# Down-projection of both gated layers by seven products instead of eight blocks, and another bank for the third pair

## The chip, the cores and the metric

One core of a Trainium2 chip runs the whole program. Its engines are a matrix engine (TensorE, PE in the rows, with PEld for its weight loads), VectorE (DVE), ScalarE (ACT), GpSimd (POOL), and SyncE (SP), which here only issues transfers. Each takes its own list of instructions in order. Transfers go through sixteen DMA engines. The metric is the time of one execution on the device, in microseconds.

## What is computed

A trunk of two layers over a sequence of 1024 rows of 1024 numbers, all in float32. Each layer is a mixer and then a gated feed-forward part; only the latter is changed:

```python
def conv_ffn(hn, w_in, conv_w, conv_b, w_out):      # D_FF = 2816
    a, u = jnp.split(hn @ w_in, 2, axis=-1)
    a = lax.conv_general_dilated(a, conv_w[:, None, :], ...) + conv_b   # causal, width 3
    return (jax.nn.silu(a) * u) @ w_out
...
h = h + mix(rmsnorm(h, norm_mix_g[layer]))
h = h + conv_ffn(rmsnorm(h, norm_ffn_g[layer]), ...)
return rmsnorm(h, final_norm_g)                      # after both layers
```

## The kernel before

**Precision.** Every float32 operand is split in two parts of a shorter type, hi on ScalarE (L129) and lo = x − hi on VectorE (L130). A product is then three matmuls (`mm3`, L161 to L163): hi·hi, hi·lo, lo·hi, each 128 x 128 stationary against 128 x 512 moving.

**Up-projection.** The 2816 columns are taken as 22 tiles of 128; for each, `Pair(f)` holds the a and the u half. It is one level of Strassen's scheme (seven products a11, s2, a12, s3, s1, a22, s4 instead of eight), each product four k times three matmuls. The weight's sums s1 to s4 are made by GpSimd (L880 to L886) in the loaded tile "raw"; each operand is then split into a tile of the ring "op" (six tiles of 1024 columns), three products ahead of use (`LOOK`). The results meet in three PSUM banks a pair, X, Y and Z; VectorE adds them up (L911, L915, L925, L932), convolves (L1068, L1070), ScalarE applies SiLU, and `tail` multiplies (L933 on VectorE, L934 on GpSimd) and writes the tile to `g_dram`. The first three pairs start early: while the second half of the rows is normalized and transposed, the matrix engine runs their a11 and a12. Their banks are written out by hand; bank 0 is X of pair 0 and also Z of pair 2.

**Down-projection.** The tiles of g are read back in groups of four (the first group two), split, and multiplied with the matching rows of w_out by `down`: for each group eight row blocks times two column halves, each block a PSUM bank "row" added into h by VectorE (L1092). In the last group the order is by row block, so that a block's two halves are done one after the other; in the last layer `final` then normalizes that row block and writes it out.

**Order.** A scheduler with a model of time lays out each engine's list; what it gives is shown below where it matters. SyncE's list holds all loads and writes of this stage.

Of the kernel before, what the change touches and what calls it, by code (L numbers as in the profile page):

```python
# [12 lines left out]
F32 = mybir.dt.float32  # L13
# [7 lines left out]
P = 128  # L21
# [23 lines left out]
LOOK = 3  # L45
EL, OL = (1, 2), (1, 3)
# [10 lines left out]
class Trunk:  # L57
# [11 lines left out]
    def weights(self, raw=0, bufs=0, size=1024):  # L69

        with self.tc.tile_pool(name="w", bufs=1, reuse_waits="tile") as w:
# [6 lines left out]
                "op": [base("whi", WBUFS) + base("wlo", WBUFS), 0],  # L78
# [742 lines left out]
    def ffn(self, L, h, pool, final=None):  # L821
# [10 lines left out]
        g_dram = tc.dram_tile([NF, P, S], F32, name="g_dram")  # L832
# [97 lines left out]
        def tail(p):  # L930
# [4 lines left out]
            nc.sync.dma_start(out=g_dram[p.f], in_=ct)  # L935
# [65 lines left out]
        ring = [[5, 3, 1, 6, 4, 2, 7, 0], 0]  # L1001
# [6 lines left out]
        for p, y, z in zip(early, (5, 6, 7), (3, 4, 0)):  # L1008
            p.banks = {"Y": y, "Z": z}
# [26 lines left out]
        for i, (p, name) in enumerate(steps):  # L1036
# [5 lines left out]
            run(p, name)  # L1042
            left[p.f] -= 1
# [4 lines left out]
        group = []  # L1048
        for f in range(0, NF, 2):
            gt = self.slot(("hn", "hn", "g", "g", "g")[f // 2 % 5], [P, 2, 2, S], F32R, name="g")  # L1050
            for m in range(2):
                ct = self.wtile("raw", F32) if f == 0 else pool.tile([P, S], F32, tag="ct", name="gr")
                nc.sync.dma_start(out=ct, in_=g_dram[f + m])
                self.split(gt[:, m, 0], gt[:, m, 1], ct)
            group += [(gt[:, m, 0], gt[:, m, 1]) for m in range(2)]
            done = f == NF - 2
            if len(group) == 4 or f == 0:
                f0 = f + 2 - len(group)
                self.down(h, group, w_out[f0 * P:(f + 2) * P], done, final() if done and final is not None else None)
                group = []  # L1060
# [12 lines left out]
    def down(self, h, x, w, last, final):  # L1073

        nc = self.nc
        nk = len(x)

        def chunks(col):
            cols = slice(col * HALF, (col + 1) * HALF)
            return [  # L1080
                self.weight(w[k0 * P:(k0 + 2) * P, cols].rearrange("(k p) n -> p k n", p=P)) for k0 in range(0, nk, 2)
            ]

        def block(half, t, col, wts):
            acc = self.bank(name="row")
            c0 = half * HALF + t * P
            for k in range(nk):
                self.mm3(
                    acc, [v[:, c0:c0 + P] for v in x[k]], [v[:, k % 2] for v in wts[k // 2]], k == 0, k == nk - 1
                )  # L1090
# [489 lines left out]
```

## Time and profile before

| | |
|---|---|
| median of 3 runs | 2330.0 us (2328.97 to 2330.22) |
| the profiled execution | 2328.61 us, span of its records 2326.6 us |
| PE busy | 2253.3 us, 97% |
| VectorE, ScalarE, GpSimd busy | 66%, 37%, 23% |
| DMA | 208.05 MB, mean 89 GB/s |

The two microseconds between execution and span lie before the first and behind the last record. The up-projections run from about 459 to 901 us and from 1623 to 2065 us, the down-projections from there to 1153 and 2312 us.

### The profile page before, as it was taken

The page shows a single profiled execution, that of the slowest core. Times are in us where ns is not written, and L with a number is a line of the kernel's source. Part 1 is how long each engine was busy: PE and PEld are TensorE (multiplying, and loading weights), DVE is VectorE, ACT ScalarE, POOL GpSimd, SP SyncE. Part 2 cuts the span into 40 slices and gives each one's busy share as a digit, 9 for nine tenths or more (in the row PEclk, how much of TensorE's full clock was granted, in tenths as well). Part 3 has the DMA queues.
Part 4 walks back from the last instruction along what each step waited for, and adds up shares of the span by engine and source line. Part 5 has one row for each costly group of instructions (what it writes and reads, how often), then busy time and mean ns, then how long its engine had stood idle before and what let it go on. Part 6 is the DMA issues. An engine that isn't in the chain of part 4 may idle for free. (4 is left out here: it accounts for less than half of the span.)

```text
span 2326.6 us, 29393 instructions
## 1 busy us (share of the span) xinstructions
PE 2253.3 (97%) x10945; PEld 1857.8 (80%) x10945; DVE 1541.0 (66%) x2627; ACT 860.9 (37%) x1498; POOL 535.1 (23%) x509
## 2 busy tenths in 40 slices
PE   7999999989999999999989999999899999999997
PEld 6777878868888887888888888887688888878886
DVE  6878895777666667544467777748776666665435
ACT  5454553443333333211234555545433333332112
POOL 0466410224444441000001000001344444410000
PEclk9999999989999999999999999999999999999999
DMA  6432323322222224321301000242222222243201
GB/s 195 126 106 80 105 91 109 127 64 82 82 82 82 82 82 159 130 92 61 113 10 45 30 31 27 109 156 73 64 90 81 80 81 80 83 169 127 91 28 73
DMA packets 196310, 208.05 MB, mean 89 GB/s; under 512 B 28289, under 2 KB 152393, under 8 KB 195657
## 3 DMA queue, kind: packets, MB, share of 16 engines
q1 hardware_dynamic: 196168, 206.19, 27.3%
q8 instruction: 86, 1.41, 0.2%
q14 instruction: 56, 0.45, 0.1%
HBM read 165.39 MB, written 39.58 MB: 88 GB/s over the span
## 5 line engine op out<-in xcount | busy, mean ns | idle before, releaser
L130 DVE TENSOR_TENSOR op<-raw,op 128x512 fp32r<-128x512 f32 x260 | 229.8, 886 | 213.3 <-ACT op L129 211.4
L161 PE MATMUL au<-bt,op 128*128 128x512 f32 x704 | 280.7, 399 | 16.7 <-DVE ct L933 12.4
L129 ACT ACTIVATE whi<-raw 128x1024 fp32r<-128x1024 f32 (+4 forms) x143 | 143.3, 1004 | 402.5 <-PE row L163 290.0
L162 PE MATMUL au<-bt,op 128*128 128x512 f32 x704 | 280.1, 398 | 1.4 <-DVE bt L130 1.4
L163 PE MATMUL au<-bt,op 128*128 128x512 f32 x704 | 279.6, 397 | 0.0
L162 PE MATMUL row<-wlo,g 128*128 128x512 f32 x704 | 275.8, 392 | 1.4 <-DVE wlo L130 1.3
L163 PE MATMUL row<-whi,g 128*128 128x512 f32 x704 | 274.8, 390 | 0.0
L129 ACT ACTIVATE op<-raw 128x512 fp32r<-128x512 f32 x260 | 163.0, 629 | 299.8 <-PE au L163 185.2
L161 PE MATMUL row<-whi,g 128*128 128x512 f32 x704 | 266.8, 393 | 1.3 <-DVE p L932 1.3
L130 DVE TENSOR_TENSOR wlo<-raw,whi 128x1024 fp32r<-128x1024 f32 (+4 forms) x143 | 171.7, 1201 | 114.3 <-ACT whi L129 113.7
L1092 DVE TENSOR_TENSOR h<-h,row 128x512 f32<-128x512 f32 x192 | 129.9, 684 | 173.5 <-PE row L163 173.2
L163 PE MATMUL au<-b,op 128*128 128x512 f32 x528 | 208.0, 394 | 1.1 <-DVE op L130 1.1
L161 PE MATMUL au<-b,op 128*128 128x512 f32 x528 | 208.0, 394 | 0.0
L162 PE MATMUL au<-b,op 128*128 128x512 f32 x528 | 207.9, 394 | 0.0
L161 PEld LDWEIGHTS au<-bt,op 128*128 128x128 f32 x704 | 133.5, 190 | 51.8 <-DVE ct L933 13.3
L162 PEld LDWEIGHTS au<-bt,op 128*128 128x128 f32 x704 | 133.7, 190 | 34.1 <-DVE bt L130 2.3
L163 PEld LDWEIGHTS au<-bt,op 128*128 128x128 f32 x704 | 133.6, 190 | 32.2
L161 PEld LDWEIGHTS row<-whi,g 128*128 128x128 f32 x704 | 132.1, 188 | 31.1 <-DVE p L932 2.2
L162 PEld LDWEIGHTS row<-wlo,g 128*128 128x128 f32 x704 | 132.2, 188 | 30.9 <-DVE wlo L130 2.9
L163 PEld LDWEIGHTS row<-whi,g 128*128 128x128 f32 x704 | 132.2, 188 | 29.8
L880 POOL TENSOR_TENSOR s<-raw 128x512 f32<-128x512 f32 x44 | 60.0, 1365 | 260.2 <-DMA raw<-in_ffn_w_in 229.0
L163 PEld LDWEIGHTS au<-b,op 128*128 128x128 f32 x528 | 99.0, 188 | 24.6 <-DVE op L130 1.4
(596 smaller groups left out, 4853.2 us busy)
## 6 DMA issues: line engine op xcount, KB each, us to landing
raw<-in_ffn_w_in SPq DMA_DIRECT2D x176, 256.0 KB, 3.1
g_dram<-ct SPq DMA_DIRECT2D x44, 512.0 KB, 3.4
raw<-in_ffn_w_out SPq DMA_DIRECT2D x44, 512.0 KB, 3.6
raw<-in_even_w_in SPq DMA_DIRECT2D x40, 512.0 KB, 3.8
gr<-g_dram SPq DMA_DIRECT2D x40, 512.0 KB, 3.2
h<-in_x SPq DMA_DIRECT2D x16, 512.0 KB, 10.4
raw<-in_even_w_out SPq DMA_DIRECT2D x16, 512.0 KB, 3.7
raw<-in_odd_w_out SPq DMA_DIRECT2D x16, 512.0 KB, 4.0
```

Of the source, the lines that this page charges most:

```text
L129: nc.scalar.activation(hi, src, AF.Copy)
L130: nc.vector.tensor_tensor(out=lo, in0=src, in1=hi.bitcast(F32), op=ALU.subtract)
L161: mm(out, l[0], r[0], start=start, stop=False, **how)
L162: mm(out, l[0], r[1], start=False, stop=False, **how)
L163: return mm(out, l[1], r[0], start=False, stop=stop, **how)
L880: tt(out=s.s1, in0=p("a21"), in1=p("a22"), op=ALU.add)
L1092: nc.vector.tensor_tensor(out=part, in0=part, in1=acc, op=ALU.add)
```

## The change

**Down-projection.** It becomes one level of the same scheme. g is cut by row halves (lo, hi) and by even and odd column tiles; w_out by even and odd row tiles and by column halves. Seven products take the place of eight blocks. Each runs over eleven steps q (two tiles f each), four row tiles t and the three matmuls of `mm3`: 132 matmuls and four banks. Four products accumulate on banks that others began; VectorE adds the banks to the quarters of h (L1153), 36 additions a layer.

**Operands of g.** `tail` now writes, for every two tiles, seven pieces of 128 x 512 to `g_dram`: three as they are and the sums s1 to s4 that VectorE makes (four operations of 128 x 512).

**Operands of w_out.** `turned(q)` loads two rows of tiles of 512 KB (buffers b1, which takes the place of the norm's gain row, and b2), makes four differences in place on VectorE (L964), and writes four pieces of 256 KB to a new DRAM tile `t_dram`. It is called eleven times in a layer, within the up-projection, in program order spread over its pairs (`TURN`).

**Streaming.** Each step of each product loads its two operands (256 KB each) into a half of a tile of a ring "row" and splits 128 x 1024 at once into one of fourteen units of memory; 77 such steps a layer. Nothing stays in memory from product to product.

**Buffers and banks.** The ring "op" has five tiles instead of six, since b2 takes one. Pair 2 has banks 5 and 7 instead of 7 and 0 for Y and Z, and the ring of banks for the pairs after it has another order.

**Final norm.** Its sums of squares are kept for each half and row tile, since the quarters of h are done in another order: the second half's left columns after the third product, the first half's two after the sixth, the second half's right columns after the seventh.

```diff
+TURN = (4, 6, 7, 8, 10, 12, 14, 15, 16, 18, 20)
...
-                "op": [base("whi", WBUFS) + base("wlo", WBUFS), 0],
+                "op": [base("whi", WBUFS) + base("wlo", WBUFS - 1), 0],
+                "row": [base("raw", WRAW) + more("raw+", raw) + base("whi", WBUFS) + base("wlo", WBUFS), 0],
...
-            nc.sync.dma_start(out=g_dram[p.f], in_=ct)
+            q, odd = p.f // 2, p.f % 2
+            put = lambda i, x: nc.sync.dma_start(out=g_dram[q, i], in_=x)
+            put(odd, ct[:, hi])
+            if not odd:
+                return
+            put(2, ct[:, lo])
+            even = pairs[p.f - 1].ct
+            s1, s2 = piece("p16", 2), piece("p16", 2)
+            V.tensor_tensor(out=s1, in0=even[:, lo], in1=ct[:, lo], op=ALU.add)
+            put(3, s1)
+            V.tensor_tensor(out=s2, in0=s1, in1=even[:, hi], op=ALU.subtract)
+            put(4, s2)
+            s3 = piece("s1", 2)
+            V.tensor_tensor(out=s3, in0=even[:, hi], in1=even[:, lo], op=ALU.subtract)
+            put(5, s3)
+            s4 = piece("u3", 1)
+            V.tensor_tensor(out=s4, in0=ct[:, hi], in1=s2, op=ALU.subtract)
+            put(6, s4)
+
+        def turned(q):
+
+            b1 = self.const.tile([P, S], F32, tag="gain", name="b1", bufs=1)
+            b2 = self.w.tile([P, S], F32, tag=f"wlo{WBUFS - 1}", name="b2", bufs=1)
+            for i, x in enumerate((b1, b2)):
+                nc.sync.dma_start(out=x, in_=w_out[(2 * q + i) * P:(2 * q + i + 1) * P])
+            sub = lambda out, x, y: V.tensor_tensor(out=out, in0=x, in1=y, op=ALU.subtract)
+            sub(b1[:, lo], b1[:, hi], b1[:, lo])
+            sub(b1[:, hi], b2[:, hi], b1[:, hi])
+            sub(b2[:, hi], b2[:, hi], b1[:, lo])
+            sub(b2[:, lo], b2[:, lo], b2[:, hi])
+            for i, x in enumerate((b1[:, lo], b2[:, hi], b1[:, hi], b2[:, lo])):
+                nc.sync.dma_start(out=t_dram[q, i], in_=x)
...
-        ring = [[5, 3, 1, 6, 4, 2, 7, 0], 0]
+        ring = [[3, 0, 6, 4, 1, 7, 5, 2], 0]
...
-        for p, y, z in zip(early, (5, 6, 7), (3, 4, 0)):
+        for p, y, z in zip(early, (5, 6, 5), (3, 4, 7)):
...
+            if name == "a12" and p.f in TURN:
+                turned(TURN.index(p.f))
...
-            if len(group) == 4 or f == 0:
-                f0 = f + 2 - len(group)
-                self.down(h, group, w_out[f0 * P:(f + 2) * P], done, final() if done and final is not None else None)
-                group = []
...
+        self.down(h, g_dram, t_dram, w_out, final() if final is not None else None)
...
-        if LASTMAJ and last:
-            both = [chunks(col) for col in range(2)]
-            for half in range(2):
-                for t in range(TB):
-                    for col in range(2):
-                        block(half, t, col, both[col])
-        else:
-            for col in range(2):
-                wts = chunks(col)
-                for half in range(2):
-                    for t in range(TB):
-                        block(half, t, col, wts)
...
+    def down(self, h, g, turned, w, final):
+
+
+        nc, tc = self.nc, self.tc
+        V = nc.vector
+        nq = NF // 2
+        low = [(x, n) for tag, k in (("hn", 2), ("g", 3)) for x in [tag] * k for n in range(2)]
+        own = [(f"b{i}", 0) for i in range(2, 6)]
+        units = {True: low + own, False: low[4:] + own}
+        held, at, last = {}, [0], []
+
+        def unit(free):
+
+            ring = units[free]
+            tag, n = ring[at[0] % len(ring)]
+            at[0] += 1
+            shape = [P, 2, 2, HALF]
+            if tag[0] == "b":
+                return self.xp.tile(shape, F32R, tag=tag, name="unit", bufs=1)
+            if n == 0:
+                held[0] = self.slot(tag, [P, 2] + shape[1:], F32R, name="unit")
+            return held[0][:, n]
+
+        def operands(q, a, b, free):
+            r = self.wtile("row", F32)
+            nc.sync.dma_start(out=r[:, :HALF], in_=g[q, a])
+            if isinstance(b, tuple):
+                src = w[(2 * q + b[0]) * P:(2 * q + b[0] + 1) * P, b[1] * HALF:(b[1] + 1) * HALF]
+            else:
+                src = turned[q, b]
+            nc.sync.dma_start(out=r[:, HALF:], in_=src)
+            u = unit(free)
+            flat = lambda x: x.rearrange("p s n -> p (s n)")
+            self.split(flat(u[:, 0]), flat(u[:, 1]), r)
+            return u
+
+        def product(banks, a, b, start, free, tail):
+            us = []
+            order = [(q, t) for q in range(nq - tail) for t in range(TB)]
+            order += [(q, t) for t in range(TB) for q in range(nq - tail, nq)]
+            for q, t in order:
+                while len(us) < min(nq, q + 9):
+                    us.append(operands(len(us), a, b, free))
+                u = us[q]
+                with tc.issue_after(last[0].ins) if last else nullcontext():
+                    mm = self.mm3(
+                        banks[t], [u[:, i, 0, t * P:(t + 1) * P] for i in range(2)], [u[:, i, 1] for i in range(2)],
+                        start and q == 0, q == nq - 1, skip_group_check=not start,
+                    )
+                last[:] = [mm]
+
+        def add(banks, *to, done=()):
+            for t in range(TB):
+                for half, col in to:
+                    x = h[half][:, t, col * HALF:(col + 1) * HALF]
+                    V.tensor_tensor(out=x, in0=x, in1=banks[t], op=ALU.add)
+                for half, col in done if final is not None else ():
+                    final(h[half], half, t, col)
+
+        banks = lambda: [self.bank(name="row") for _ in range(TB)]
+        X, Y = banks(), banks()
+        product(X, 0, (0, 0), True, True, 3)
+        add(X, (1, 1), (0, 0), (0, 1))
+        product(Y, 4, 1, True, True, 3)
+        add(Y, (1, 1))
+        product(X, 1, (1, 0), False, True, 3)
+        add(X, (1, 0), done=[(1, 0)])
+        product(Y, 5, 2, False, True, 3)
+        add(Y, (0, 1))
+        X = banks()
+        product(X, 3, 0, True, True, 3)
+        add(X, (0, 1))
+        product(Y, 2, 3, False, True, 3)
+        add(Y, (0, 0), done=[(0, 0), (0, 1)])
+        at[0] = 0
+        product(X, 6, (1, 1), False, False, 7)
+        add(X, (1, 1), done=[(1, 1)])
```

**What the lists look like.** VectorE's list about the third pair's first sums, in layer 0, before (L911 and L932 add a PE bank to a piece p, L130 splits an operand of the up-projection):

```order
L911 TENSOR_TENSOR p_4763<-p_4340,au 128x512
L130 TENSOR_TENSOR op<-raw,op 128x512
L1070 SCALAR_TENSOR_TENSOR ct<-ax,taps,ct 128x1024
L932 TENSOR_TENSOR p_4763<-p_4763,au 128x512
L130 TENSOR_TENSOR op<-raw,op 128x512
L933 TENSOR_TENSOR ct<-ct,au 128x512
L915 TENSOR_TENSOR u_4801<-p_4340,au 128x512
L130 TENSOR_TENSOR op<-s_4721,op 128x512
L130 TENSOR_TENSOR op<-raw,op 128x512
L925 TENSOR_TENSOR ax<-p_4340,au 128x512
```

and after (L915 and L936 are the same two additions, L964 is a difference of `turned`, its b a tile just loaded from w_out, L955 the last sum of `tail`):

```order
L955 TENSOR_TENSOR u_4757<-ct,p_4749 128x512
L964 TENSOR_TENSOR b_5980<-b_5980 128x512
L915 TENSOR_TENSOR p_4777<-p_4341,au 128x512
L936 TENSOR_TENSOR p_4777<-p_4777,au 128x512
L964 TENSOR_TENSOR b_5980<-b_5981,b_5980 128x512
L964 TENSOR_TENSOR b_5981<-b_5981,b_5980 128x512
L964 TENSOR_TENSOR b_5981<-b_5981 128x512
L919 TENSOR_TENSOR u_4815<-p_4341,au 128x512
L132 TENSOR_TENSOR op<-raw,op 128x512
L132 TENSOR_TENSOR op<-s_4722,op 128x512
```

Four differences now stand between the pair's additions, and the first of them, which needs a load, stands ahead of L915. The scheduler has drawn the calls forward: all 44 differences of a layer stand between the second half's norm and the sixth pair's sums (places 704 to 846 of VectorE's list in layer 0, 1900 to 2042 in layer 1), 5 of them ahead of the first pair's L915 in layer 0, and 13 in layer 1. On SyncE's list their loads and writes stand between the loads of w_in of the same pairs.

VectorE's list about the change from one pair to the next, in the later part of the up-projection, before (L933 is the last multiplication of a pair, L911 the first addition of the next pair, behind its product s2, and L915 the one behind its s3):

```order
L130 TENSOR_TENSOR op<-raw,op 128x512
L933 TENSOR_TENSOR ct<-ct,au 128x512
L911 TENSOR_TENSOR p_5849<-p_5831,au 128x512
L130 TENSOR_TENSOR op<-raw,op 128x512 x2
L915 TENSOR_TENSOR u_5887<-p_5831,au 128x512
L130 TENSOR_TENSOR op<-raw,op 128x512 x2
```

and after, at a change from an odd pair to an even one (L937, L915 and L919 are the same three; L947, L949 and L955 are sums of `tail`):

```order
L937 TENSOR_TENSOR ct<-ct,au 128x512
L947 TENSOR_TENSOR p_5609<-ct 128x512
L132 TENSOR_TENSOR op<-raw,op 128x512
L949 TENSOR_TENSOR p_5610<-p_5609,ct 128x512
L955 TENSOR_TENSOR u_5618<-ct,p_5610 128x512
L132 TENSOR_TENSOR op<-raw,op 128x512
L915 TENSOR_TENSOR p_5658<-p_5640,au 128x512
L919 TENSOR_TENSOR u_5708<-p_5640,au 128x512
```

The next pair's first addition, which came right behind the multiplication, now stands behind three sums and two splits of operands, right ahead of the second addition. It also has a new wait: its piece p (tag "p16", two buffers) is the one from which the sum s1 of L947 is written to `g_dram`, and L915 waits for that write to land. Splits of operands on ScalarE (L131) wait for a free tile of "op": with five tiles, for the end of the product five ahead of the one whose operand is split. The split in front of L915 here is that of a11 of the pair after; its tile is the one that the running pair's a12 uses. So stands the list at seven changes in layer 0 (into pairs 8 to 20) and eight in layer 1 (into 6 to 20); at the one into pair 6 of layer 0 the second split stands ahead of L955.

VectorE's list at the end of layer 0's down-projection before (L204 is the next layer's norm of the first two row tiles, L1092 the additions of the last row blocks):

```order
L181 TENSOR_SCALAR vu<-vt 128x2
L182 TENSOR_TENSOR vt<-vt,vu 128x2
L183 SCALAR_TENSOR_TENSOR vy<-vt,vy 128x2
L204 SCALAR_TENSOR_TENSOR xn<-h,vy,gain 128x1024 x2
L1092 TENSOR_TENSOR h<-h,row 128x512 x3
L130 TENSOR_TENSOR hn_lo<-tps,hn_hi 128x4x128
L1092 TENSOR_TENSOR h<-h,row 128x512
L130 TENSOR_TENSOR wlo<-raw,whi 128x640
L130 TENSOR_TENSOR hn_lo<-tps,hn_hi 128x4x128 x2
```

and after, from the additions of the sixth product on (L1153; the unit rows are splits of the seventh product's operands, ang the rotary angles, wlo the splits of the mixer's first weights):

```order
L1153 TENSOR_TENSOR h<-h,row 128x512
L132 TENSOR_TENSOR unit<-row,unit 128x1024 x4
L1153 TENSOR_TENSOR h<-h,row 128x512 x4
L174 TENSOR_SCALAR v _9188<-ss 128x2
L1243 TENSOR_TENSOR ang<-freq,pos 128x8x32
L175 TENSOR_SCALAR vy<-v _9188 128x2
L1253 TENSOR_SCALAR ang<-ang 128x8x32
L178 TENSOR_TENSOR vt<-vy 128x2
```

and fourteen rows further on in the same list:

```order
L184 TENSOR_TENSOR vt<-vt,vu 128x2
L132 TENSOR_TENSOR wlo<-raw,whi 128x768
L185 SCALAR_TENSOR_TENSOR vy<-vt,vy 128x2
L1266 TENSOR_SCALAR ang<-ang 128x8x32
L132 TENSOR_TENSOR wlo<-raw,whi 128x768
L206 SCALAR_TENSOR_TENSOR xn<-h,vy,gain 128x1024 x2
L132 TENSOR_TENSOR wlo<-raw,whi 128x640 x2
```

Before, the norm's xn stood ahead of the last four additions; now the last four additions (L1153 x4) stand ahead of the whole norm, and nine angle operations and four splits of 128x768 stand between.

## Rows read from the trace of the kernel before

**Rows 1.** The page's part 1: busy time, share of the span, instructions.

```profile
PE 2253.3 (97%) x10945; PEld 1857.8 (80%) x10945; DVE 1541.0 (66%) x2627; ACT 860.9 (37%) x1498; POOL 535.1 (23%) x509
```

**Rows 2.** The page's part 5: line engine operation out<-in, count | busy, mean | idle before.

```profile
L162 PE MATMUL row<-wlo,g 128*128 128x512 f32 x704 | 275.8, 392 | 1.4 <-DVE wlo L130 1.3
```

**Rows 3.** Windows: start:end length, busy and count of PE PEld DVE ACT POOL, clock, DMA.

```profile
700.00:800.00 100.00, 100.00 (x431) 80.57 (x431) 62.97 (x76) 31.97 (x51) 42.15 (x37) 1.00 0.27 88
1000.00:1100.00 100.00, 100.00 (x438) 82.06 (x437) 45.43 (x62) 16.70 (x18) 0.00 (x0) 1.00 0.25 80
2075.00:2095.00 20.00, 20.00 (x90) 16.38 (x89) 16.05 (x22) 7.93 (x8) 0.14 (x1) 1.00 0.61 208
```

**Rows 4.** Waits of the matrix engine: total us, times, longest us.

```profile
PE tps L210 <- DVE xn L204: 14.2, 2, 9.0
PE au L161 <- DVE ct L933: 12.4, 2, 6.4
```

**Rows 5.** Windows of the wait in layer 0's early up-projection.

```profile
511.30:517.30 6.00, 0.07 (x1) 0.00 (x0) 4.75 (x6) 1.69 (x2) 2.95 (x3) 0.91 0.28 83
517.30:521.00 3.70, 3.68 (x9) 2.90 (x10) 0.00 (x0) 0.00 (x0) 1.71 (x2) 0.50 0.31 125
```

**Rows 6.** Window from the second half's norm to the sixth column tile, layer 0.

```profile
478.60:601.00 122.40, 113.33 (x469) 90.12 (x468) 88.73 (x101) 42.33 (x62) 50.54 (x40) 0.94 0.26 81
```

**Rows 7.** VectorE, window 478.6:601, grouped by line and shape.

```profile
L130 DVE TENSOR_TENSOR op<-raw,op 128x512 fp32r<-128x512 f32 x33 | 28.9, 878 | 24.4 <-ACT op L129 24.3
```

**Rows 8.** Timeline of VectorE near 495: start, us, engine, line, operation, count.

```profile
495.00 1.29 DVE L130 TENSOR_TENSOR op<-raw,op 128x512 fp32r<-128x512 f32 x2
```

**Rows 9.** The DMA view: issues, count, KB each, median us to landing.

```profile
raw<-in_ffn_w_out SPq DMA_DIRECT2D x44, 512.0 KB, 3.6
...
trunk_out<-o SPq DMA_DIRECT2D x16, 256.0 KB, 2.0
```

**Rows 10.** Timeline of VectorE about the end of one pair of layer 0.

```profile
737.51 0.69 DVE L933 TENSOR_TENSOR ct<-ct,au 128x512 f32<-128x512 f32 x1 [0.26 <-ACT ct L1071]
738.21 0.69 DVE L911 TENSOR_TENSOR p<-p,au 128x512 f32<-128x512 f32 x1
...
741.74 1.31 DVE L130 TENSOR_TENSOR op<-raw,op 128x512 fp32r<-128x512 f32 x1 [2.11 <-ACT op L129]
743.81 0.69 DVE L915 TENSOR_TENSOR u<-p,au 128x512 f32<-128x512 f32 x1 [0.76 <-PE au L163]
```

**Rows 11.** Timeline of ScalarE and of GpSimd at the same place.

```profile
741.07 0.63 ACT L129 ACTIVATE op<-raw 128x512 fp32r<-128x512 f32 x1 [2.18 <-POOL raw L884]
...
741.21 1.29 POOL L880 TENSOR_TENSOR s<-raw 128x512 f32<-128x512 f32 x1 [0.22 <-DMA raw<-in_ffn_w_in]
```

**Rows 12.** Timeline of the matrix engine at a wait of layer 1, and the window behind.

```profile
1650.94 0.47 PE L161 MATMUL au<-bt,op 128*128 128x512 f32 x1 [2.33 <-DVE b L130]
...
1650.90:1653.00 2.10, 2.06 (x9) 1.74 (x10) 2.10 (x2) 0.00 (x0) 0.00 (x0) 1.00 0.00 0
```

**Rows 13.** Timeline of layer 0's end: VectorE and the matrix engine.

```profile
1143.80 2.48 DVE L204 SCALAR_TENSOR_TENSOR xn<-h,vy,gain 128x1024 f32<-128x1024 f32 x2
...
1152.63 0.39 PE L163 MATMUL row<-whi,g 128*128 128x512 f32 x1
1152.86 0.34 PE L161 MATMUL low<-whi,hn_hi 128*128 128x384 f32 x1
```

**Rows 14.** VectorE, window 1100:1185, by line and shape; and tile ang.

```profile
L130 DVE TENSOR_TENSOR wlo<-raw,whi 128x1024 fp32r<-128x1024 f32 x3 | 3.7, 1224 | 3.6 <-ACT whi L129 3.6
L130 DVE TENSOR_TENSOR wlo<-raw,whi 128x768 fp32r<-128x768 f32 x2 | 1.9, 960 | 5.0 <-ACT whi L129 5.0
...
L1189 DVE SCALAR_TENSOR_TENSOR ang<-ang x3: 419/425/425, 1073.0 to 1074.4; 128x256 f32<-128x256 f32 x3
```

**Rows 15.** Timeline of the end of the span: matrix engine, then VectorE.

```profile
2311.97 0.39 PE L163 MATMUL row<-whi,g 128*128 128x512 f32 x1
...
2321.99 1.41 DVE L1516 SCALAR_TENSOR_TENSOR o<-h,vy,gain 128x512 f32<-128x512 f32 x2
```

More of the change, by code (lines that the diff above doesn't have):

```diff
@@ L831, in ffn @@
         g_row = self.gain(self.a["norm_ffn_g"][L:L + 1])
-        g_dram = tc.dram_tile([NF, P, S], F32, name="g_dram")
+        g_dram, t_dram = (
+            tc.dram_tile([NF // 2, n, P, HALF], F32, name=name) for n, name in ((7, "g_dram"), (4, "t_dram"))
+        )
         KH = KD // 2
@@ L1047, in ffn @@
         self.psum(mm=8)
-        group = []
[L1049 to L1056, printed above, removed]
-            if len(group) == 4 or f == 0:
-                f0 = f + 2 - len(group)
-                self.down(h, group, w_out[f0 * P:(f + 2) * P], done, final() if done and final is not None else None)
-                group = []
+        self.down(h, g_dram, t_dram, w_out, final() if final is not None else None)
     def conv(self, out, ax, taps, f, span):
@@ L1071, in conv @@
         nc.scalar.activation(t, t, AF.Silu)
[L1073 to L1090, printed above, removed]
-            part = h[half][:, t, col * HALF:(col + 1) * HALF]
-            nc.vector.tensor_tensor(out=part, in0=part, in1=acc, op=ALU.add)
-            if final is not None:
-                final(h[half], half, t, col)
-        if LASTMAJ and last:
-            both = [chunks(col) for col in range(2)]
-            for half in range(2):
-                for t in range(TB):
-                    for col in range(2):
-                        block(half, t, col, both[col])
-        else:
-            for col in range(2):
-                wts = chunks(col)
-                for half in range(2):
-                    for t in range(TB):
-                        block(half, t, col, wts)
@@ new lines, in down @@
+    def down(self, h, g, turned, w, final):
[40 more added lines that the diff above has]
+                        start and q == 0, q == nq - 1, skip_group_check=not start,
+                    )
+                last[:] = [mm]
[24 more added lines that the diff above has]
+        add(X, (1, 1), done=[(1, 1)])
@@ L1504, in after @@
             if col == 0:
-                ss[t] = pool.tile([P, 2], F32, tag="fss", name="fss", bufs=4)
+                ss[half, t] = pool.tile([P, 2], F32, tag="fss", name="fss", bufs=8)
             junk = pool.tile([P, S + 2], F32, tag="ax", name="fj", bufs=1)[:, :HALF]
-            nc.scalar.activation(junk, h[:, t, cols], AF.Square, accum_out=ss[t][:, col:col + 1])
+            nc.scalar.activation(junk, h[:, t, cols], AF.Square, accum_out=ss[half, t][:, col:col + 1])
             if col == 0:
                 return
-            s = ss[t]
+            s = ss[half, t]
             nc.vector.tensor_tensor(out=s[:, 0:1], in0=s[:, 0:1], in1=s[:, 1:2], op=ALU.add)
```

## The prediction

> **What bounds the kernel now.** First the page's busy times: the matrix engine works 97% of the span, 73 us short of it [rows 1]. So time is saved by fewer matmuls, or in those 73 us. The groups by cost come next: the matmuls into "row" banks are three lines of 704, one of them shown, 2112 or 1056 a layer [rows 2]. Their mean of 392 ns isn't their price, since matmuls overlap; that is read from a window without a wait. From 1000 to 1100 us 438 ran in 100 us of busy time, 228.4 ns each; in the up-projection 431, 232 ns [rows 3]. The list of waits then shows where the matrix engine stands: 14.2 us for the norm's xn, and 12.4 us in two for ct L933, pair 0's last use of bank 0, which pair 2's Z needs [rows 4]. That wait is longer than it looks: in the 3.7 us behind it the granted clock is 0.50, the 1.2 GHz level, half the work [rows 5]. The last view is of the neighbours: from the second half's norm to the sixth column tile VectorE is busy 88.7 of 122.4 us [rows 6], and there the change puts work.
>
> **1. Fewer matmuls.** Seven products of 132 are 924 a layer instead of 1056; 264 go in all. 264 x 0.2284 = **−60.3 us** (the sizes stay, so I keep the pace).
>
> **2. Streaming.** A layer loads 77 x 512 KB = 40.4 MB in 924 x 0.2284 = 211 us, 191 GB/s. The trace shows 208 GB/s at a DMA share of 0.61 while the matrix engine was busy throughout [rows 3]. Splits take 1.22 us on VectorE [rows 14]: 77 x 1.22 + 36 x 0.69 = 119 of 211 us. Loads run up to nine steps ahead, 9 x 12 x 0.228 = 25 us, against 3.6 us for 512 KB [rows 9]. Hence **0**; below nothing, above rival B.
>
> **3. The early up-projection.** Removed, per layer: some 6 us of wait and 1.85 us lost to the half clock behind it. Added on VectorE: 44 differences and twelve sums, 56 operations of 128x512. Two of this shape back to back took 1.29 us [rows 8], so 36 us. They run beside GpSimd: a split of this shape takes 0.69 alone [rows 8, 10], 0.878 as a mean here [rows 7]; 56 times the difference is 10 us. Then the differences wait in line for loads. One round of `turned` is four differences (2.6 us), the last piece's write (nearest row: 256 KB, 2.0 us) and the next load (3.6) [rows 9], 8.2 us, and eleven are 90 in some 115. So a load is mostly in time, with a margin of about 2 us; if it is late, all behind it on VectorE is, the pair's additions that free a bank above all. I take 5 us. In layer 0 five of them stand ahead of the stretch, −3. The lead of three products, 3 x 12 x 0.232 = 8.4 us, can be run down once. So 88.7 + 36 + 10 + 5 − 3 − 8.4 = 128 against 122.4, +6. In layer 1 thirteen stand ahead, −8 instead of −3, but they push into a norm for which the matrix engine waits already [rows 4]; I take +4. Together **+10 us**. Bounds: all hidden and the removed wait back, −8 a layer; every round late, rival A, up to +22.
>
> A rule of the Trainium skill speaks against these additions ("SBUF — State Buffer", section "SBUF: two separate sides"): a VectorE operation with two inputs in SBUF and a GpSimd operation that reads SBUF lock each other out for a whole instruction. The trace agrees at the one place shown: a split that began at 741.74 inside a GpSimd operation took 1.31 and ended 0.55 after it [rows 10, 11]. With GpSimd busy 50.5 of 122.4 us [rows 6], 41%, half of 1.29 for each that meets one is 15 us a layer where the means gave 10: 10 more in all, within the forecast's range.
>
> **4. The change from an odd to an even pair.** Before, L911 followed the multiplication L933 at once, 738.21, when s2's matmuls ended, and a12 (2.8 us) covered it: s3, which adds to the same bank, followed without a gap and L915 came at 743.81 behind it [rows 10]. After, this addition stands behind the split of a11 of the pair after, which ScalarE can't start before a12 has ended, since its tile is a12's. Rows of before show the place: ScalarE splits at 741.07, 0.63 us, right when a12 ends [rows 11]; VectorE's lo follows at 741.74, for 1.31 beside GpSimd (0.69 without) [rows 10]; then the addition, 0.69. s3 could start at 743.1 to 743.75 instead of 740.85 or so: 2.25 to 2.9 us in which the matrix engine has nothing, since its list is in order. The write of s1 is no later: the sum ready at 738.9, issued by 739.6 behind two others, landed 2.0 later (256 KB [rows 9]) at 741.6; only if it takes over 3 us does it decide, for some tenths. The clock: behind a wait of 2.33 us the matrix engine had 1.00 [rows 12], so nothing is added for it. I take 2.4 for each of fifteen and 1.5 for pair 6 of layer 0: **+37 us**. That is the change's second largest term. Bounds: 0 if ScalarE gets its tile earlier than I read it (rival D); 3.5 each, 54, with a late write.
>
> **5. Layer 0's end.** Before, the next layer's norm of two row tiles (xn at 1143.8) ran under the last row blocks, and the mixer's first matmul followed at 0.23 us [rows 13]. After, VectorE has it behind the last additions, and with it ten small operations of the root (2 us), nine angle operations (three at 0.425 [rows 14], others no longer; 3.5), four splits of 128x768 at 0.96 [rows 14] (3.8), and one xn of 1.24 [rows 13]. With the addition (0.7), transpose and split (1.2) that is 12.4 us with nothing ready for the matrix engine, and 1.85 for the half clock that rows 5 show behind a long wait: **+14 us**. Lower bound 8, since VectorE is then ahead for the second pair of row tiles, whose xn is waited for now [rows 4]; upper 20, since the splits go through two raw tiles, with reloads of about 3.6 us.
>
> **6. The end.** Before, VectorE came to the last row blocks with a queue: the last matmul began at 2311.97, the last o at 2321.99 [rows 15], end 2326.6, 14.4 us behind the matmuls. After, one column half of one block is left: addition 0.7, square 0.8, root 2 to 3, o 1.4, write 3.2 as now, up to 10.4 with a queue of one: **−4 us** (−3 to −6).
>
> **7. The rest at 0.** The first operands of the down-projection are read under the last pair (−1 to +4). The sums of later pairs, four in two pairs, fit beside VectorE's 63 of 100 us [rows 3], save for item 4.
>
> **Sum.** 2328.6 (span 2326.6 and two around it) − 60.3 + 10 + 37 + 14 − 4 = 2325.3. The median shown is 1.4 above the profiled execution: **2327 us**. I call 0.2%, 4.7 us, about what runs of this kernel can tell from no change, so 2327 is none that counts.
>
> **The rivals.**
> A. *VectorE becomes the bound of the first six pairs* (slower). Each round of `turned` takes 11 us instead of 8.2, so that the chain of eleven, 121 us, sets the stretch: +13 to +22 a layer in place of 5, 2343 to 2361. For: 125 of 122 us before any wait. Against: what is late is caught up in later pairs.
> B. *The down-projection follows its loads.* With one pair of loads under way, 512 KB in 3.6 us is 146 GB/s, 277 us a layer in place of 211: 2459. It decides from 191 GB/s down; at 180 it costs 13 a layer, 2353. Against: 208 was shown [rows 3].
> C. *The additions of item 3 are hidden,* and the removed wait shows in full: −8 a layer in place of 5, 2301.
> D. *Item 4 doesn't show.* The tile comes free a product earlier, the split is done, the addition finds its write landed: 2290 (faster).
>
> **How the numbers follow.** The forecast's own range, 2313 to 2341, holds 0.50; A 0.20, B 0.05, C 0.13, D 0.12. The range from 2290 to 2352 leaves out half of D, B, and a third of A. Faster: C, D and 0.21 of the forecast's lower part, 0.46; the same 0.20; slower: A, B and the upper part, 0.34.
>
> **What would show it.** Right: 1848 row matmuls of 228 ns without waits; no wait for ct; differences with means near 0.85 us; a wait of 2.2 to 2.9 us for p L915 at fifteen places, 39 us apart; a gap of 12 to 16 us ahead of low; the end 10 us behind the last matmul. Wrong: row matmuls that wait for unit (B); differences with a gap for DMA in each round (A); no wait for L915 (D); the first six pairs under 115 us (C).

## The result, and the profile after

The changed kernel takes 2399.7 us (median of 4 runs, 2399.49 to 2400.62) against 2329.5 for the kernel before, run beside it (2328.92 to 2330.22): a ratio of 1.0302, 95% interval 1.0284 to 1.032. The profiled execution has a span of 2397.8 us, 71.2 longer. So it is slower by 3%, above the range of the prediction (2290 to 2352).

The page's part 1 of the kernel after (busy time, share of the span, instructions) answers to [rows 1]:

```profile
PE 2224.4 (93%) x10681; PEld 1827.7 (76%) x10681; DVE 1680.6 (70%) x2749; ACT 925.4 (39%) x1564; POOL 544.4 (23%) x509
```

264 matmuls are gone, and yet the matrix engine's busy time fell by only 29 us; its idle time grew from 73 to 173 us. What it waits for stands in the list of waits after (total us, times, longest us), the view of [rows 4]:

```profile
PE au L163 <- DVE p L915: 95.1, 25, 17.2
PE tps L212 <- DVE xn L206: 24.6, 3, 12.3
PE au L163 <- DVE u L919: 7.0, 3, 3.9
PE row L163 <- DVE p L936: 5.1, 2, 2.8
```

The wait for ct is gone, and one for VectorE's addition L915 has come, 25 times, 95.1 us. (L915 is the addition behind a pair's product s2, L911 before; L919 the one behind s3; L936 is the last addition of a pair; L163 to L165 are `mm3`.) The timeline of the matrix engine after (start, us, line, operation, in brackets the idle time before it and what ended it) tells the short waits from the long:

```profile
545.67 0.80 PE L163 MATMUL au<-bt,op 128*128 128x512 f32 x1 [17.23 <-DVE p L915]
...
590.98 0.79 PE L163 MATMUL au<-bt,op 128*128 128x512 f32 x1 [8.24 <-DVE p L915]
...
643.66 0.80 PE L163 MATMUL au<-bt,op 128*128 128x512 f32 x1 [10.13 <-DVE p L915]
...
686.47 0.51 PE L163 MATMUL au<-bt,op 128*128 128x512 f32 x1 [2.09 <-DVE p L915]
...
729.53 0.50 PE L163 MATMUL au<-bt,op 128*128 128x512 f32 x1 [2.09 <-DVE p L915]
...
771.05 0.51 PE L163 MATMUL au<-bt,op 128*128 128x512 f32 x1 [2.09 <-DVE p L915]
...
1183.44 0.40 PE L165 MATMUL row<-unit 128*128 128x512 f32 x1
...
1196.18 1.97 PE L212 MATMUL tps<-ident,xn 128*128 128x128 f32 x8 [12.35 <-DVE xn L206]
...
1755.37 0.80 PE L163 MATMUL au<-bt,op 128*128 128x512 f32 x1 [13.01 <-DVE p L915]
...
2388.58 0.40 PE L165 MATMUL row<-unit 128*128 128x512 f32 x1
```

From the change into pair 8 on (in layer 1 from the one into pair 6) there is a wait of 2.09 us at each change from an odd to an even pair, seven in layer 0 and eight in layer 1, 31.4 us. They are item 4 of the prediction. The idle time isn't their whole price: two pairs now take 41.52 us (729.53 to 771.05), and before they took 39.13, from L911 at 738.21 [rows 10] to this row of VectorE's timeline before:

```profile
777.34 0.69 DVE L911 TENSOR_TENSOR p<-p,au 128x512 f32<-128x512 f32 x1
```

Before these fifteen, in the first pairs, stand waits of up to 17 us: 40.2 us in layer 0 with the smaller ones and those for L919, 30.5 in layer 1. Against these the prediction had the 5 us a layer of item 3 for late loads.

Where the 71.2 us lie follows from four instants. Layer 0's last row matmul moved from 1152.63 [rows 13] to 1183.44, by 30.8; its down-projection is 30.2 shorter (half of item 1), so the up-projection ahead of it grew by 61.0 (counting in the wait at the start of the down-projection, one of the two for L936). The end of layer 0 grew by 14.9. In layer 1 the last row matmul moved from 2311.97 [rows 15] to 2388.58, by 76.6: less the 30.8 and the 14.9, and with 30.2 of its own down-projection, its up-projection grew by 61.1. What follows it shrank from 14.6 to 9.2 us, by 5.4.

How the longest wait comes about is seen on VectorE. Its timeline after, about that wait, and about a later change of pair:

```profile
535.39 3.07 DVE L964 TENSOR_TENSOR b<-b,b 128x512 f32<-128x512 f32 x2 [1.49 <-DMA b<-in_ffn_w_out]
538.39 0.67 DVE L937 TENSOR_TENSOR ct<-ct,au 128x512 f32<-128x512 f32 x1
538.99 1.15 DVE L964 TENSOR_TENSOR b<-b 128x512 f32<-128x512 f32 x1
540.06 0.68 DVE L947 TENSOR_TENSOR p<-ct 128x512 f32<-128x512 f32 x1
...
543.57 0.69 DVE L964 TENSOR_TENSOR b<-b 128x512 f32<-128x512 f32 x1 [1.30 <-DMA b<-in_ffn_w_out]
544.92 0.69 DVE L915 TENSOR_TENSOR p<-p,au 128x512 f32<-128x512 f32 x1 [0.67 <-DMA g_dram<-p]
...
642.92 0.69 DVE L915 TENSOR_TENSOR p<-p,au 128x512 f32<-128x512 f32 x1 [4.25 <-DMA g_dram<-p]
...
723.97 0.69 DVE L937 TENSOR_TENSOR ct<-ct,au 128x512 f32<-128x512 f32 x1 [0.25 <-ACT ct L1096]
724.69 1.16 DVE L947 TENSOR_TENSOR p<-ct 128x512 f32<-128x512 f32 x1
...
728.18 0.69 DVE L132 TENSOR_TENSOR op<-raw,op 128x512 fp32r<-128x512 f32 x1 [0.40 <-ACT op L131]
728.79 0.68 DVE L915 TENSOR_TENSOR p<-p,au 128x512 f32<-128x512 f32 x1
```

The sums s1 and s2 are written from pieces p of tag "p16", which has two buffers, and the next pair's L915 wants one of them. So this addition can't run until the pair before is wholly done: its multiplication (L937), its sum s1 (L947), and the write of s1. In the early pairs, which overlap, that stretches far. Ahead of L937 stand two differences with a late load in front (1.49 us), between it and L915 two more with another (1.30), and then the write, for 0.67. At 642.92 the write alone holds L915, and all of VectorE with it, for 4.25 us. At 728.79, later on, the order is the one that the prediction describes: multiplication, sums, a split that waits for ScalarE, L915; no write is late there, and the price is that of the order.

SyncE's timeline after shows the writes that these two wait for (start, us, line, transfer):

```profile
539.51 0.40 SPq L963 DMA_DIRECT2D b<-in_ffn_w_out  x1
...
540.77 0.32 SPq L940 DMA_DIRECT2D g_dram<-p  x1
...
638.37 1.50 SPq L940 DMA_DIRECT2D g_dram<-p  x2
```

Issued at 540.77, let go at 544.92: 4.15 us; issued at 638.37, let go at 642.92: 4.55. The prediction took 2.0 [rows 9]. VectorE's own list of waits after holds both, the loads of w_out and the writes of the sums, for the whole kernel:

```profile
DVE b L964 <- DMA b<-in_ffn_w_out: 38.1, 25, 4.1
...
DVE u L919 <- DMA g_dram<-u: 17.7, 5, 4.1
...
DVE p L915 <- DMA g_dram<-p: 6.7, 3, 4.3
```

The DMA view after (issues, KB each, median us to landing) has the spread:

```profile
b<-in_ffn_w_out SPq DMA_DIRECT2D x44, 512.0 KB, 3.9
...
g_dram<-ct SPq DMA_DIRECT2D x66, 256.0 KB, 2.1
...
g_dram<-p SPq DMA_DIRECT2D x44, 256.0 KB, 3.2
...
g_dram<-u SPq DMA_DIRECT2D x22, 256.0 KB, 4.4
```

The windows after (start:end, length; busy and count of PE, PEld, DVE, ACT, POOL; granted clock, DMA share, GB/s):

```profile
481.00:601.00 120.00, 88.07 (x335) 68.44 (x336) 99.40 (x115) 30.66 (x44) 41.14 (x30) 0.83 0.66 218
545.60:549.00 3.40, 3.33 (x8) 2.67 (x9) 0.70 (x2) 0.00 (x0) 0.00 (x0) 0.50 0.82 274
686.40:689.00 2.60, 2.53 (x8) 2.06 (x9) 0.02 (x1) 0.00 (x0) 0.80 (x2) 0.73 0.73 240
729.50:732.00 2.50, 2.47 (x11) 2.02 (x12) 0.00 (x0) 0.00 (x0) 0.73 (x1) 1.00 0.70 216
975.00:1184.00 209.00, 208.28 (x915) 171.68 (x915) 110.33 (x113) 73.56 (x76) 6.22 (x3) 1.00 0.55 189
```

In the early 120 us, 335 matmuls ran where 469 had run in 122.4 [rows 6]. The 335 took 88.1 us busy, 7 more than at the pace of [rows 6]; the granted clock was 0.83 against 0.94 there, and 0.50 behind the longest wait. The down-projection's 915 recorded matmuls were busy for 208.3 of 209 us, at 189 GB/s: it is what was promised.

### The profile page after: what moved, and what is told of

Its sections match the earlier page's. It is cut to its first block, busy times and chain, and to the rows that moved or that the text cites. A ratio compares the mean times of both kernels' runs of the same rounds, so it can differ in the third digit from the quotient of the medians.

```text
span 2397.8 us, 30063 instructions
## 1 busy us (share of the span) xinstructions
PE 2224.4 (93%) x10681; PEld 1827.7 (76%) x10681; DVE 1680.6 (70%) x2749; ACT 925.4 (39%) x1564; POOL 544.4 (23%) x509
## 5 line engine op out<-in xcount | busy, mean ns | idle before, releaser
L163 PE MATMUL au<-bt,op 128*128 128x512 f32 x704 | 292.9, 416 | 108.8 <-DVE p L915 95.1
L132 DVE TENSOR_TENSOR op<-raw,op 128x512 fp32r<-128x512 f32 x260 | 241.0, 928 | 113.0 <-ACT op L131 111.3
L131 ACT ACTIVATE op<-raw 128x512 fp32r<-128x512 f32 x260 | 162.4, 628 | 388.0 <-PE au L165 326.8
L164 PE MATMUL au<-bt,op 128*128 128x512 f32 x704 | 288.6, 410 | 2.8 <-DVE bt L132 2.8
L165 PE MATMUL au<-bt,op 128*128 128x512 f32 x704 | 288.1, 409 | 0.0
L132 DVE TENSOR_TENSOR unit<-row,unit 128x1024 fp32r<-128x1024 f32 x154 | 184.0, 1229 | 132.6 <-ACT unit L131 129.2
L163 PEld LDWEIGHTS au<-bt,op 128*128 128x128 f32 x704 | 138.8, 197 | 155.3 <-DVE p L915 104.5
L131 ACT ACTIVATE unit<-row 128x1024 fp32r<-128x1024 f32 x154 | 155.6, 1053 | 234.7 <-PE row L165 178.8
L163 PE MATMUL row<-unit 128*128 128x512 f32 x616 | 240.9, 391 | 5.1 <-DVE p L936 5.1
L164 PE MATMUL row<-unit 128*128 128x512 f32 x616 | 240.6, 391 | 0.0
L165 PE MATMUL row<-unit 128*128 128x512 f32 x616 | 240.6, 391 | 0.0
L165 PE MATMUL au<-b,op 128*128 128x512 f32 x528 | 208.7, 395 | 1.1 <-DVE op L132 1.1
L163 PE MATMUL au<-b,op 128*128 128x512 f32 x528 | 208.7, 395 | 0.0
L164 PEld LDWEIGHTS au<-bt,op 128*128 128x128 f32 x704 | 139.4, 198 | 35.9 <-DVE bt L132 3.6
L165 PEld LDWEIGHTS au<-bt,op 128*128 128x128 f32 x704 | 138.8, 197 | 34.2
L132 DVE TENSOR_TENSOR wlo<-raw,whi 128x1024 fp32r<-128x1024 f32 (+4 forms) x99 | 118.3, 1196 | 59.9 <-ACT whi L131 59.3
L131 ACT ACTIVATE whi<-raw 128x1024 fp32r<-128x1024 f32 (+4 forms) x99 | 96.8, 981 | 138.9 <-PE row L165 60.6
L163 PEld LDWEIGHTS row<-unit 128*128 128x128 f32 x616 | 116.0, 188 | 30.4 <-DVE p L936 6.0
L165 PEld LDWEIGHTS row<-unit 128*128 128x128 f32 x616 | 116.0, 188 | 24.6
L164 PEld LDWEIGHTS row<-unit 128*128 128x128 f32 x616 | 116.1, 188 | 24.5
```

The source lines that it names most:

```text
L131: nc.scalar.activation(hi, src, AF.Copy)
L132: nc.vector.tensor_tensor(out=lo, in0=src, in1=hi.bitcast(F32), op=ALU.subtract)
L163: mm(out, l[0], r[0], start=start, stop=False, **how)
L164: mm(out, l[0], r[1], start=False, stop=False, **how)
L165: return mm(out, l[1], r[0], start=False, stop=stop, **how)
```

## The experiments

Two theories of the 61 us in each up-projection. *Buffers*: the sums that are being written to DRAM hold pieces that the next pair's additions want. *Crowding*: the 44 differences, drawn forward into the first six pairs with their loads and writes, make VectorE late; what it waits for is then only a form of that. Every edit below is to the changed kernel, unless it says otherwise. The scheduler lays out the lists anew for each, so a difference in time holds the new order too.

**In place.** s1 and s2 overwrite the even tile's halves, s3 is made first; no piece of "p16" is written out any more.

```diff
-            s1, s2 = piece("p16", 2), piece("p16", 2)
+            s3 = piece("s1", 2)
+            V.tensor_tensor(out=s3, in0=even[:, hi], in1=even[:, lo], op=ALU.subtract)
+            put(5, s3)
+            s1, s2 = even[:, lo], even[:, hi]
...
```

> The sums s1 and s2 of g are written over the even tile's two halves, so that no piece p is shared with them. First theory: of the 95 us that the matrix engine waits for p L915, only the fifteen waits of 2.09 in the later pairs and some 2 each in the early ones are owed to the shared piece and to the split ahead of it; the long early ones (17.2, 8.2, 10.1, 13.0, 8.4) are owed to the differences of turned crowded into the first six pairs. Then 33 to 42 us come back, 2358 to 2367. Rival: the write of s1 is behind all of them; then some 95 come back, about 2305.

**No differences.** `turned` is left out, the down-projection loads untreated rows of w_out.

```diff
-            if name == "a12" and p.f in TURN:
-                turned(TURN.index(p.f))
...
-                src = turned[q, b]
+                src = w[2 * q * P:(2 * q + 1) * P, :HALF]
```

> turned is left out, and products that would read its pieces read a half of w_out instead, so that the result isn't the product; matmuls, streaming and the sums of g stay. First theory: the early stretch falls back by about 40 us a layer, 2315 to 2325, with the waits of 2.09 still there. Rival (the write of s1): the long waits of pairs 2, 4 and 6 stay, 2370 to 2385.

**Spread.** The differences of call q are held behind the addition L929 of the pair TURN[q] − 1 (`marks` keeps that instruction).

```diff
+            with tc.issue_after(marks[TURN[q] - 1].ins):
                 sub(b1[:, lo], b1[:, hi], b1[:, lo])
...
```

> The differences of each turned are held behind the addition L929 of the pair ahead of its place in TURN, so that they are spread over the up-projection. First theory: the crowding is gone, and four differences in two pairs fit VectorE's idle time: 2315 to 2335. Rival (the write of s1, or the work itself wherever it stands): 2370 or more.

**Both**, in place and spread.

> Sums in place and differences spread. First theory: all of the up-projection's waits but those of its start are gone, 2280 to 2295, faster than before by 35 to 50. Rival: if only one of the two mattered, no more than the better of the two runs above.

Measured on one chip, before at 2328.4: in place 2354.4 (ratio 1.0107, 1.0092 to 1.0122), no differences 2344.7 (1.0068, 1.0053 to 1.0083), spread **2431.7** (1.045, 1.0433 to 1.0468), both 2416.7 (1.038, 1.0365 to 1.0396). Each edit alone takes away part: 45 and 55 us. All four missed the numbers of the first theory, by 4, 20, 97 and 122 us; of the rivals' numbers only that of "spread" (2370 or more) was met. In place, no wait of 2.09 us is left in the later pairs; without differences they stay: item 4 belongs to the shared piece. That spreading costs 32 us more and "both" 62 more than "in place" follows from neither theory. The list of waits of the in-place kernel shows what took over:

```profile
PE au L163 <- DVE u L919: 53.6, 19, 14.2
```

It is the fourth sum. s4 lies in tag "u3", which has one buffer, and L919 of the next pair needs it. I had left it at 0, in item 7. In the kernel with both edits SyncE's and VectorE's timelines show its price when a load of `turned` goes just ahead of it:

```profile
618.03 0.39 SPq L965 DMA_DIRECT2D b<-in_ffn_w_out  x1
...
619.63 0.33 SPq L942 DMA_DIRECT2D g_dram<-u  x1
```

```profile
625.25 0.69 DVE L921 TENSOR_TENSOR u<-p,au 128x512 f32<-128x512 f32 x1 [0.99 <-DMA g_dram<-u]
```

5.6 us from issue to the addition (L921 is L919 there). The lists of waits have this for the whole of it, the matrix engine's and VectorE's:

```profile
PE au L163 <- DVE u L921: 105.0, 22, 8.0
```

```profile
DVE u L921 <- DMA g_dram<-u: 42.3, 19, 3.3
```

And VectorE's in the kernel that is only spread (L917 is L915 there):

```profile
DVE p L917 <- DMA g_dram<-p: 35.3, 18, 3.4
```

Crowded into the first pairs, the differences disturb six pairs; spread, their transfers stand ahead of such writes all along the up-projection. So spreading hurts as long as the writes are waited for. VectorE's waits for them bear that out: 42.3 us in 19 for s4's write against 6.1 in 6 with the sums in place and the differences crowded, and 35.3 in 18 for s1's against the 6.7 in 3 above. That it is the loads of `turned` that make them late is seen at the one place shown.

In the kernel without differences the longest wait, on the matrix engine's timeline, is at the same place as the 17.23:

```profile
533.78 0.80 PE L163 MATMUL au<-bt,op 128*128 128x512 f32 x1 [9.86 <-DVE p L915]
```

So at this place some 9.9 us come from the shared buffer alone, and 7.4 from the differences on top.

**A piece of its own for s4**, in tag "p1" with three buffers, with s1 and s2 in place: spread, and as placed by the scheduler.

```diff
-            s4 = piece("u3", 1)
+            s4 = piece("p1", 3)
```

> As the run with sums in place and differences spread, and s4 has a buffer of the tag p1 instead of the pair's only u. There the matrix engine waited 105.0 us in 22 for u L919, and VectorE ahead of it for the landing of the write of s4 from that buffer (5.6 us from issue, behind other transfers). If the shared buffer is the cause, those waits go, and with them some 1.85 us of half clock behind each: 2416.7 - 105 - 40, 2265 to 2290, faster than before. If the spread differences themselves hold VectorE up, no lower than 2340.

> As the run with sums in place, with the differences crowded as the scheduler put them, and s4 in a buffer of its own (tag p1). 53.6 us of waits for u L919 stood there. If they are owed to the landing of s4's write, 2300 to 2320. If VectorE is full and waits in line for loads of w_out in the first six pairs, most of it stays: 2335 to 2354.

Measured, before at 2328.8: 2364.8 (1.0145, 1.0124 to 1.0166) and 2365.3 (1.016, 1.0146 to 1.0173). The second lies above both of its expectations; the first lies where its rival had it (no lower than 2340). In both the wait moved to the next user of the buffer that s4 now shares, not because a write is late: neither ScalarE nor VectorE has a wait for a write of a sum there. Where the copy is late, it stands right behind a split on ScalarE's list (at 736.12 in the first, the copy after a split at 735.60). That user is ScalarE's copy of a pair's first product into p1 (L909 here, L911 in the first); the list of waits of the second:

```profile
PE au L163 <- ACT p L909: 37.4, 18, 5.6
...
PE au L163 <- DVE u L919: 16.7, 8, 5.5
```

**The bank alone.** The kernel before, with only the third pair's banks and the new ring.

```diff
-        ring = [[5, 3, 1, 6, 4, 2, 7, 0], 0]
+        ring = [[3, 0, 6, 4, 1, 7, 5, 2], 0]
-        for p, y, z in zip(early, (5, 6, 7), (3, 4, 0)):
+        for p, y, z in zip(early, (5, 6, 5), (3, 4, 7)):
```

> The kernel before with nothing but the other banks of pair 2 and the other ring. If no wait takes the place of the two for ct L933 (12.4 us and 3.7 of half clock behind them), 2310 to 2316; if the next wait in line (VectorE's last additions, or a bank of the ring) comes a few us later, 2320 to 2328.

2317.4 against 2328.8 (0.9948, 0.9936 to 0.9961): 11.4 us gained, a little short of the 2310 to 2316 expected. Its list of waits begins with the norm's xn (14.2 us) as before, and has no wait for ct and nothing new in its place. That is some 70% of the 16 us that the prediction put on the removed wait and the half clock behind it in the two layers.

**Layer 0's end.** The kernel with s4 in "p1" and differences as placed; the last product's additions, the angles and the mixer's first weights are held behind the first xn of the next norm (`mark`).

```diff
+                        with tc.issue_after(mark):
+                            self.late()
...
+            with tc.issue_after(mark):
                 cos, sin = self.rope_tables(tp)
```

> As the run with the crowded differences and s4 in its own buffer, and at the end of layer 0 the last product's additions, the angles and the splits of 128x768 are held behind the first norm of two row tiles on VectorE, so that this norm runs under the last product. If VectorE's list was the cause of the 12.4 us gap ahead of the mixer, 8 to 12 us less than the run without it, and a gap of 1 to 3 us in its place; if the transposes or the weights can't come earlier, no change.

2354.8 against 2365.3 without it, 10.5 us gained, within the 8 to 12 expected (`late` holds the last product's additions). The list of waits has xn with 11.4 us in two instead of 24.8 in three; the 12.4 are gone.

**s4 in tag "p5"**, two buffers, with the mended end: as placed, and spread.

```diff
-            s4 = piece("p1", 3)
+            s4 = piece("p5", 2)
```

> As the last run, but s4 has the tag p5 (two buffers, the next use of its buffer a pair and a half later) instead of p1; the differences stay crowded. In the last run 36.2 us of waits stood at ACT p L911: the copy of the next p1 shares its ring with s4, and ScalarE's list has it behind a split that waits for the matrix engine. If shared buffers are all that the waits in the later pairs are made of, these go in full and only the first six pairs keep some: 2300 to 2320. If the crowded differences were the greater part, 2335 or more.

> As the run above, with the differences spread over the up-projection. If the sums' buffers were what made spreading dear (105 us of waits in the first run with it), nothing is left between the early pairs and the end of the up-projection, and the kernel gains what fewer matmuls give: 2329 - 60 - 16 (bank) + 3 to 8 at layer 0's end - 5 at the end, 2250 to 2275. If VectorE's 56 operations a layer cost time wherever they stand, 2300 or more.

Measured, before at 2329.7: 2311.2 (0.9919, 0.9906 to 0.9933) and **2287.2** (0.9819, 0.9805 to 0.9833). The first is within what was expected (2300 to 2320). The second beats both kernels, by 42.6 and some 112 us. With free buffers spreading gains 24 us, where with shared ones it had cost 32, and with s4 in "p1" it changed nothing (2364.8 against 2365.3). No wait of VectorE for a load of w_out or for a write of the sums is left in it. It misses its own expectation by 12 us: the list of waits and the window 700:800 of this kernel show what is left (L919 there is L915 of the kernel after):

```profile
PE au L163 <- DVE p L919: 22.9, 24, 2.5
```

```profile
700.00:800.00 100.00, 97.54 (x416) 77.55 (x415) 78.31 (x95) 31.53 (x50) 43.97 (x35) 1.00 0.49 155
```

VectorE has 78 of 100 us there instead of 63 [rows 3], and 24 waits of a mean of 0.95 us remain, spread over the pairs.

**Evener calls.** The same with TURN = (3, 5, 7, 9, 11, 13, 15, 17, 19, 20, 21).

> As the fastest run, with the eleven calls one in two pairs (TURN 3, 5, ... 19, 20, 21), each behind L929 of an even pair, so that no two stand in neighbouring pairs and none directly ahead of an odd pair's four sums. The fastest run has 22.9 us of waits for the first addition of a pair, the longest 2.5 where two calls are neighbours. If VectorE's load by pair makes them, 2270 to 2282; if the differences delay the convolution of whatever pair they stand in, no change or some us more.

**Buffers alone.** The changed kernel with nothing but s1 and s2 in place and s4 in "p5".

> The changed kernel with nothing but the three buffers of the sums moved: s1 and s2 over the even tile's halves, s4 under the tag p5; the differences crowded and the end of layer 0 as they were. If sharing buffers with writes is the greater part of what went wrong, about 2322 (the 2311 of the run with the end of layer 0 mended, and 10.5 for that end); if the mended end did more than it seemed to, 2330 to 2345.

Measured, before at 2330.4: evener calls 2286.8 (0.9809, 0.9793 to 0.9824), the same as without; buffers alone 2318.7 (0.9946, 0.9929 to 0.9962). The evener calls do take away half of the small waits:

```profile
PE au L163 <- DVE p L919: 10.8, 16, 1.5
```

VectorE is as full there (78.9 of the 100 us from 700 to 800), so its load as such doesn't make these waits; where the calls stand does. What is gained goes in part at the starts of the down-projections: from the last matmul of the up-projection to the last row matmul the two layers take 429.7 us instead of 422.5.

Buffers alone is the cleanest: three buffers moved (and s3 made first), 81 us gained, the change turned from 3% slower to 0.5% faster, near the 2322 expected. Its list of waits:

```profile
PE au L163 <- DVE p L915: 21.9, 12, 5.5
PE au L163 <- DVE u L919: 11.8, 6, 4.1
```

None of these is at a later change of pair: the last in layer 0 is at 648.5 us, the last in layer 1 at 1810.6. The fifteen waits of 2.09 are gone too. On VectorE no wait for a write of the sums is left, but that for the loads is, nearly in full:

```profile
DVE b L964 <- DMA b<-in_ffn_w_out: 31.9, 19, 2.6
```

## Why the prediction was wrong

| term | predicted | measured |
|---|---|---|
| 1, fewer matmuls | −60.3 | as taken |
| 2, streaming | 0 | 0: 208.3 of 209.0 us busy |
| 3, early up-projection, both layers | +10 | about +77, what is left |
| 4, odd to even pair | +37 | about +45 |
| 5, end of layer 0 | +14 | +14.9 |
| 6, the end | −4 | −5.4 |
| 7, the rest | 0 | not apart from 3 |
| sum | −3.3 | +71 |

**Item 3 failed.** Both up-projections grew by 122 us together; less item 4, 77 are left, with the one place (the change into pair 6 of layer 0) that item 4 had at 1.5. Its working counted operations on VectorE and loads of `turned`, and gave the pairs' additions no other cause for being late. Two of its steps failed. The first is the 5 us a layer for late loads, worked out from a round of 8.2 us: VectorE waited 38.1 us for loads of w_out in the two layers (not all of which the matrix engine felt). The second is a wait put at nothing. The sums of `tail` stood at 0 in item 7, "save for item 4". But the mechanism of item 4, an addition that can't start before a sum is made and written from its piece, holds in the early pairs as well, and there more stands between: pairs overlap, the sums come late, and the writes land after 4.2 and 4.6 us at the two places shown instead of 2.0. And the piece of s4, one buffer, wasn't looked at. The buffers took 81 us in all (buffers alone), of which item 4 is 45; so some 36 of the 77 are theirs. The other 41 remain with the buffers free. Spreading takes 24 of these (s4 in "p5", spread against as placed), and with them the waits for loads: that is crowding, rival A's mechanism. About 17 stay in the best kernel. It has 22.9 us in 24 small waits for L915; how these, the clock behind them and what the bank change gives back make up the 17 was not measured apart. These shares are one way through the edits; with shared buffers spreading has the other sign, so they don't hold in any order.

**Item 4 was right in place, count and cause, and its size was a little low.** The order of VectorE's list at 723.97 to 728.79 is the one described. At most of the fifteen places two pairs take 41.52 us against 39.13 before, 2.4 more, as taken (against 38.92 in layer 1, 2.6). The clock, taken at nothing, costs some more: at four of the thirteen intervals between these waits it is 43.06 (686.47 to 729.53, against 729.53 to 771.05). From the first wait to the last are 252.2 us in layer 0, where six times 39.13 are 234.8, and 293.6 in layer 1, where seven times 38.92 are 272.4: 38.6 more in thirteen intervals, some 45 for fifteen. That the list stands so at all is due to the shared piece: with the buffers moved, no such wait is left.

**The others.** Items 1 and 2 held, and rival B didn't come: no row matmul waits for its unit (the 5.1 us of L936 at the two starts were 1.3 before). Item 5 held: 12.35 us for xn, and the deferred additions, angles and splits give 10.5 of it back. Item 6 was a little better than taken. Rival C's gain exists (the bank alone, 11.4 us), but not in company. Rival D didn't come. Rival A had the right sign, and its own mechanism, VectorE crowded by the differences, cost 24 us by the last comparison, just under its 26 to 44 in the two layers; but it left the buffers out as the forecast did, and so ended at 2361 at most.

**The lock.** Some of the crowd's operations took 1.5 to 1.8 us, where 0.69 is the time of one alone, as the two at 535.39 (3.07 together; GpSimd worked without a break from 533.72 to 539.59); the differences of two tiles had a mean of 1042 ns in the window 481:601, the splits 918, against 878 before [rows 7]. VectorE's groups by line and shape there, after:

```profile
L964 DVE TENSOR_TENSOR b<-b,b 128x512 f32<-128x512 f32 x18 | 18.8, 1042 | 7.3 <-DMA b<-in_ffn_w_out 7.1
...
L132 DVE TENSOR_TENSOR op<-raw,op 128x512 fp32r<-128x512 f32 x23 | 21.0, 918 | 0.4 <-ACT op L131 0.4
```

The rule of the Trainium skill that the prediction cites ("SBUF — State Buffer", section "SBUF: two separate sides") that a VectorE operation with two inputs in SBUF and a GpSimd operation that reads SBUF lock each other out, fits these two: the second ended at 538.46, 0.54 us behind one of GpSimd's that ended at 537.92. By the means it is a small part of the 61 us: the 41 operations took 39.8 us in layer 0's window, 11.5 more than at 0.69 each.

## What to carry to other kernels

A buffer shared with a write to DRAM is a wait for whoever uses it next: price it by when its contents are made, by the order that this forces on the list, and by the write's landing in that stage (here 4.2 and 4.6 us where a row from elsewhere had 2.0), and do so at every place where the buffer comes round, for every buffer that the change shares. A mechanism found at one stage is to be looked for in the stages with another order, above all where pairs overlap. Spreading work with transfers helped here only once nobody waited for transfers behind them: free the buffers first, then spread; in that order, and with the end of layer 0 mended, the change is worth 1.8%.

## What was not expected of the hardware

Writes of 256 KB landed after 2.1 us for ct and 4.4 for u in the same kernel, as medians; what sets them apart was not tried. Behind waits of the same length, 2.09 us, the granted clock was 0.73 in one window (686.4 to 689.0) and 1.00 in the next (729.5 to 732.0), and the distance between the waits changed by 1.54 us with it. What tells the two places apart was not tried.
